# 48 gate tiles as 24 pairs of seven block products, computed ahead of attention and kept in DRAM

## The chip, the cores and the metric

The kernel runs on one core of a Trainium2 chip. What counts is the device time of one execution in microseconds (us); the time before is the median of three runs. Durations of single instructions come from one profiled execution.

## What is computed

One step of a hybrid decoder layer for 512 tokens of a prompt and 64 sample tokens (8 sequences of 8), which share all weights. Everything is float32. Cut to what matters here:

```python
h = _rmsnorm(x, norm_w)
u = jnp.einsum('bld,de->ble', h, w_in)         # D_MODEL = 2048 rows, all projections at once
z = u[..., OFF_Z:OFF_XBC]                      # 4096 columns
...                                            # xbc (6144), dt (64), q (2048), k and v (512 each)
g_attn = u[..., OFF_GA:OFF_MIX_S]              # 2048 columns
mix_s, mix_a = ...                             # 2048 columns each
y = _gated_group_rmsnorm(ssd(conv(xbc), dt), z, ssm_norm_w)   # y * silu(z), then a norm by group
p_ssm = y @ w_ssm_branch
o = sink_attention(q, k, v, bias) * jax.nn.silu(g_attn)
p_attn = o @ w_attn_branch
merged = jax.nn.sigmoid(mix_s) * p_ssm + jax.nn.sigmoid(mix_a) * p_attn
x = x + merged @ w_out                         # then a last rmsnorm
```

So z and g_attn are used only through a SiLU, at the end of the state-space part and of attention. Of the input projection's columns, z and g_attn are 48 tiles of 128.

## The kernel before

Tokens lie along the free dimension: 576 columns, in two halves of TH = 288. A projection tile has 128 output columns; its weights, 2048 rows, come in two chunks of 8 k-tiles (128x8x128, 512 KB, loaded by SyncE in L63 into `raw`, two buffers). `Weights.split` makes two parts of a chunk that TensorE takes at full rate, whose sum is the float32 value: `wh` by ScalarE (L70) and `wl` by VectorE (L71), three buffers each. The activations are kept in such parts too (`ah`, `al`). For each k-tile, `step` in `run_main` issues three products (wh with ah, wh with al, wl with ah) on two token halves: 6 matmuls of 288 columns, 96 a tile, all in L338, each half onto a PSUM bank of its own (`ps` in pool `pm`, two buffers of two banks).

`run_main` walks a list of tiles. After each k-tile it calls `pump`, which lets one step of the oldest generator in `quick` and one of the oldest in `jobs` issue its instructions. In this way attention (`attn_job`, about 117 steps for one of four rounds of eight heads), the convolution and the state-space groups (`ssd_job`) run between the matmuls of the projections: the engines' order is the order in which these steps are issued. If the list ends first, `drain` runs the rest without matmuls beside it.

The order of tiles: four of K, four of V, dt; then for each attention round m four tiles of q, some mix gates (`MIXES` = 6, 6, 6, 8) and the four attention gates ga of that round (`take_ga`, SiLU on ScalarE). The round's `attn_job` starts with its last q tile; at its end it waits for the ga tiles, multiplies on GpSimd (L551) and stores the result to `o_d` (L553). Then for each of eight state-space groups six tiles of xbc and four of z (`take_z`, L750, kept in SBUF as `zs`), the six mix gates that are left, and after these the output projections of the two branches and `w_out` (two parts of 320 and 256 tokens).

In a block of `attn_job`, the scores (L493) are reduced with the bias by VectorE (L497), the maximum is negated (`nm`, L504), ScalarE takes eight exponentials (L509), VectorE scales by the sum (L516), and TensorE transposes the result (L526) for the product with V (L536). Tables and constants, among them the bias expanded to DRAM (`bias_d`, eight issues of GpSimd in L370) and copies of the two caches (L409), are set up at the start, and their transfers run during K and V.

Of the kernel before, what the change touches and what calls it, by code (L numbers as in the profile page):

```python
# [16 lines left out]
P = 128  # L17
# [28 lines left out]
MIXES = (6, 6, 6, 8)  # L46
# [8 lines left out]
class Weights:  # L55
    """Weight tiles of 8 k-tiles x 128 columns, each split into two float32r parts."""
# [19 lines left out]
def hybrid(ctx, tc, x_prompt, x_sample, cache_k, cache_v, state_conv, state_ssm, norm_w, w_in, conv_w,  # L76
# [32 lines left out]
    sink_d = scratch([HEADS, 8], "sink_d")  # L109
    ea_d = scratch([H, T], "ea_d")  # L110
# [53 lines left out]
    # parameters that scale rows of transposed tiles  # L164
# [42 lines left out]
    hx, first = [act_pair(k) for k in range(KT)], []  # L207

    def to_hx(k, lo, hi, blocks):
# [43 lines left out]
    open_pools(True)  # L253

    def stat(n, name):
        return now["s"].tile([P, n], F32, tag=name, name=name)

# [1 line left out]
    pool.dma_start(out=tri, in_=c_tri)  # L259
    pool.dma_start(out=stri, in_=c_stri)  # L260
    pool.dma_start(out=own, in_=c_own)
    pool.dma_start(out=sinkb, in_=AP(sinks, 0, [[0, P], [1, HEADS]]))
    dska = kten([P, H], "dska")
    pool.dma_start(out=dska, in_=AP(d_skip, 0, [[0, P], [1, H]]))
    for hf in range(2):
        pool.tensor_copy(dsk[64 * hf:64 * hf + 64, :],
                         dska[64 * hf:64 * hf + 64].rearrange("p (t h) -> p t h", h=2)[:, :, hf])
    rb = now["s"].tile([HEADS, HEADS], F32, tag="rb", name="rb", bufs=1)
    oh = kten([P, BL], "oh")
    bd = kten([P, BL], "bd")  # L270
    pool.dma_start(out=rb, in_=rel_bias)
    pool.dma_start(out=oh[:32], in_=c_buckets)
    pool.dma_start(out=bd[:32], in_=c_band)
    pbk = bank()
    ten.matmul(pbk[:32, :BL], rb, oh[:32], start=True, stop=True)
    vec.tensor_tensor(out=oh[:32], in0=pbk[:32, :BL], in1=bd[:32], op=ALU.add)
    pool.dma_start(out=AP(biass_d, 120, [[3056, 32], [383, 8], [1, 143]]),
                   in_=AP(oh, 120, [[oh.ap[0][0], 32], [0, 8], [1, 143]]))
    sk = now["s"].tile([HEADS, 1], F32, tag="sk", name="sk", bufs=1)
    pool.dma_start(out=sk, in_=sinks.rearrange("a h -> h a"))  # L280
    sk8 = now["s"].tile([HEADS, 8], F32, tag="sk8", name="sk8", bufs=1)
    pool.tensor_copy(sk8, sk.to_broadcast([HEADS, 8]))
    pool.dma_start(out=sink_d, in_=sk8)
    for b2 in range(2):
        pool.dma_start(out=sinks_s[64 * b2:64 * b2 + 64], in_=AP(sink_d, 0, [[1, 64], [64, 4]]))

# [11 lines left out]

    def pump():
        pump_one(quick)  # L300
        pump_one(jobs)
# [9 lines left out]
    def run_main(tiles, had=()):  # L311
        """tiles: (weight loads per chunk of 8 k-tiles, act pairs, what takes the sums[, the only tokens]).
        With had, the first chunks of the first two tiles, those two tiles run side by side."""
# [11 lines left out]
        def step(n, kk, only=(0, 1)):  # L325
            i, c = flat[n]
            loads, pairs, take, *spans = tiles[i]
# [28 lines left out]

    win = w_in[0]
# [81 lines left out]
    gaT = {}  # L439
# [16 lines left out]
    def take_ga(m, r):  # L456
        def f(ps):
            gaT[m, r] = cten("ga")
            act.activation(sq(gaT[m, r]), ps[:, :, :TH], AF.Silu)
        return f  # L460

    def attn_job(m):
# [6 lines left out]
        # keys of the two kv heads, high and low parts, each twice  # L469
# [75 lines left out]
        for blk in range(4):  # L545
            yield from scores(blk)
        yield from sample_attn(m, oT)
        while (m, 3) not in gaT:
            yield
        for t in range(4):  # L550
            pool.tensor_tensor(out=oT[t], in0=oT[t], in1=gaT.pop((m, t)), op=ALU.mult)  # L551
# [113 lines left out]
        # dt in x_; dt * A, cumulated within chunks and sequences  # L665
# [11 lines left out]
        # decay to the end, times dt  # L677
# [106 lines left out]
    def ssd_job(g):  # L784
# [4 lines left out]
        # masked C.B, B by token  # L789
# [67 lines left out]
        yield from wait(2)  # L857
        yield from ssd_sample(g, xs, bT, cT)
        # gate and group norm
        tot = cten("tot")  # L860
        sqr = cten("sqr")
        for t in range(4):
            vec.tensor_tensor(out=xs[t], in0=xs[t], in1=zs.pop(4 * g + t), op=ALU.mult)  # L863
# [24 lines left out]
    def parts(dst, src, q, high, low):  # L888
        """The 32 rows of src (from partition 32 q on): high and low parts to those quarters of dst."""
# [370 lines left out]
```

## Time and profile before

| | us |
|---|---|
| median of three runs (lowest, highest) | 3341.83 (3338.98, 3344.56) |
| span of the profiled execution | 3334.8 |
| TensorE busy | 3246.0 (97%) |
| VectorE busy | 1526.2 (46%) |
| ScalarE busy | 1266.9 (38%) |
| GpSimd busy | 348.7 (10%) |

The profiled execution's own time isn't listed apart; its span runs from its first to its last instruction, and the timed runs also hold what lies around it. Shares are means over stages: the projections' matmuls run through the whole span, while attention ends at about 1106 us and the state-space groups, some 163 us each, come after it.

### The profile page before, as it was taken

Reading aid. Unit: us, or ns where it says so; the run is one execution under the profiler, and the core shown is the slowest. Engines: PE = TensorE matmul, PEld = TensorE weight load, DVE = VectorE, ACT = ScalarE, POOL = GpSimd, SP = SyncE. Lnnn points to the kernel's source line nnn. Section 1 sums busy time; section 2 is a strip of 40 time slices with the busy share of each in tenths; the row PEclk is TensorE's granted clock in tenths of the full one; section 3 lists DMA queues with packets and bytes.
Section 4 is the critical chain, followed back from the end, with each engine's and each line's share of the span. In section 5 each row is a group of like instructions: output and inputs, shape, how many; then the busy total and the mean of one; then the engine's idle time right before and its main releaser. Section 6 shows DMA issues by size and latency. Waiting matters only on the chain.

```text
span 3334.8 us, 57384 instructions
## 1 busy us (share of the span) xinstructions
PE 3246.0 (97%) x23897; PEld 3086.3 (93%) x23897; DVE 1526.2 (46%) x2881; ACT 1266.9 (38%) x2153; POOL 348.7 (10%) x423
## 2 busy tenths in 40 slices
PE   7499999999999999999999999999999999999997
PEld 6499998999999999999999898989899999999997
DVE  4044233243242375757575757575642242423544
ACT  4035335254262344444444444444431121211443
POOL 4000100100000012121212120202010000000111
PEclk9799999999999999999999999999999999999999
DMA  5933333233323344435353535353574353433555
GB/s 138 148 103 93 93 99 95 84 91 88 103 81 99 97 124 114 130 109 131 106 135 105 136 101 141 100 139 96 143 233 122 108 163 105 146 108 97 158 156 160
DMA packets 667924, 398.39 MB, mean 119 GB/s; under 512 B 31248, under 2 KB 638704, under 8 KB 667472
## 3 DMA queue, kind: packets, MB, share of 16 engines
q1 hardware_dynamic: 660800, 383.93, 40.8%
q0 software_dynamic: 6864, 10.79, 2.4%
q8 instruction: 188, 3.08, 0.4%
q14 instruction: 72, 0.59, 0.1%
HBM read 339.24 MB, written 59.29 MB: 120 GB/s over the span
## 4 chain that ended last, share of the span: by engine, by line
PE 86%; DMA 6%; POOL 3%; DVE 2%; ACT 2%; issue 1%; SPq 0%; DVEq 0%; ACTq 0%; POOLq 0%
PE ps L338 74%; PE bank L974 2%; DMA raw<-in_w_out_dram 2%; DMA raw<-in_w_in_dram 2%; PE bank L759 1%; PE bank L536 1%; POOL tot L867 1%; DMA out_dram<-knp 1%; PE bank L493 1%; PE bank L953 1%; DMA stg<-y_d 1%; POOL sqr L865 1%; PE bank L827 1%; PE bank L526 1%; DVE wl L71 1%
## 5 line engine op out<-in xcount | busy, mean ns | idle before, releaser
L338 PE MATMUL ps<-ah,wh 128*128 128x288 f32 (+2 forms) x6944 | 1568.5, 300 | 28.8 <-ACT wh L70 27.1
L338 PE MATMUL ps<-ah,wl 128*128 128x288 f32 (+2 forms) x6944 | 1554.4, 298 | 2.0 <-DVE wl L71 2.0
L338 PE MATMUL ps<-al,wh 128*128 128x288 f32 (+2 forms) x6944 | 1545.4, 297 | 0.0
L338 PEld LDWEIGHTS ps<-ah,wh 128*128 128x128 f32 x6944 | 1136.2, 190 | 65.4 <-issue 31.9
L338 PEld LDWEIGHTS ps<-ah,wl 128*128 128x128 f32 x6944 | 1138.7, 189 | 25.9 <-issue 19.9
L338 PEld LDWEIGHTS ps<-al,wh 128*128 128x128 f32 x6944 | 1138.3, 189 | 15.1 <-issue 13.2
L71 DVE TENSOR_TENSOR wl<-raw,wh 128x1024 fp32r<-128x1024 f32 x466 | 582.4, 1251 | 1107.2 <-ACT wh L70 1105.9
L70 ACT ACTIVATE wh<-raw 128x1024 fp32r<-128x1024 f32 x466 | 492.7, 1058 | 1364.6 <-PE ps L338 1125.8
L730 DVE SCALAR_TENSOR_TENSOR cacc<-craw,prm,cacc 128x600 f32<-128x600 f32 x144 | 128.5, 892 | 61.2 <-ACT cacc L728 57.8
L1179 POOL TENSOR_TENSOR res<-res,fw 128x128 f32<-128x128 f32 (+3 forms) x35 | 32.4, 949 | 856.7 <-ACT junk L1175 824.9
L968 DVE SCALAR_TENSOR_TENSOR s<-s,dec_s,bank 128x128 f32<-128x128 f32 x256 | 70.4, 343 | 59.5 <-PE bank L962 59.2
L497 DVE CUSTOM_DVE_ANT_0 sc<-bank,bm 128x256 f32<-128x256 f32 (+1 forms) x128 | 43.8, 388 | 85.0 <-PE bank L493 83.9
L773 DVE TENSOR_SCALAR L<-L,acs_n 128x128 f32<-128x128 f32 (+1 forms) x320 | 79.2, 322 | 5.9 <-DMA L<-acs_d 5.4
L1125 DVE TENSOR_TENSOR sg<-ps,sg 128x576 f32<-128x576 f32 x32 | 24.3, 758 | 124.7 <-PE ps L338 124.7
L815 POOL TENSOR_TENSOR xl<-xe,xh 128x512 fp32r<-128x512 f32 x32 | 42.2, 1320 | 260.3 <-ACT xh L814 233.2
L509 ACT ACTIVATE sc<-sc,nm 128x256 f32<-128x256 f32 (+1 forms) x128 | 60.0, 470 | 21.7 <-DVE nm L504 16.9
L865 POOL TENSOR_TENSOR tot<-xc 128x576 f32<-128x576 f32 x8 | 32.6, 4069 | 310.0 <-DVE xc L863 310.0
L974 PE MATMUL bank<-sT,cpad 128*32 128x512 f32 x128 | 61.7, 603 | 1.9 <-ACT sT L955 1.9
L955 ACT ACTIVATE sT<-bank 128x512 f32<-128x512 f32 x64 | 36.4, 598 | 68.1 <-PE bank L953 67.9
L725 POOL COPY g<-craw 128x3 f32<-128x3 f32 x48 | 38.0, 791 | 216.2 <-ACT craw L713 215.8
L541 ACT ACTIVATE oT<-bank 64x128 f32<-64x128 f32 x128 | 34.9, 272 | 46.6 <-PE bank L536 45.3
L775 ACT ACTIVATE L<-L 128x512 f32<-128x512 f32 (+1 forms) x80 | 45.2, 584 | 16.8 <-DVE L L773 15.6
(293 smaller groups left out, 2372.8 us busy)
## 6 DMA issues: line engine op xcount, KB each, us to landing
raw<-in_w_in_dram SPq DMA_DIRECT2D x306, 512.0 KB
raw<-in_w_ssm_branch_dram SPq DMA_DIRECT2D x64, 512.0 KB
raw<-in_w_out_dram SPq DMA_DIRECT2D x64, 512.0 KB
L<-acs_d SPq DMA_DIRECT2D x64, 256.0 KB
s<-in_state_ssm_dram SPq DMA_DIRECT2D x64, 256.0 KB
out_dram<-s SPq DMA_DIRECT2D x64, 256.0 KB
raw<-in_w_attn_branch_dram SPq DMA_DIRECT2D x32, 512.0 KB
y_d<-xc SPq DMA_DIRECT2D x32, 288.0 KB
```

Of the source, the lines that this page charges most:

```text
L70: pin(nc.scalar.activation(wh, raw, AF.Copy))
L71: pin(nc.vector.tensor_tensor(out=wl, in0=raw, in1=wh, op=ALU.subtract))
L338: ten.matmul(sums[i][:, s, :hi - lo], a[:, kk, :], b[:, lo:hi], start=(k == 0 and q == 0), stop=(k == last and q == 2))
L497: vec.tensor_tensor_reduce(out=s_[:, i, lo:256], in0=ps[:, i, lo:256], in1=bm[j][:, i, lo:256], scale=1.0, scalar=-3e38, op0=ALU.add, op1= ...
L509: act.activation(sc[j][:, i, lo:256], sc[j][:, i, lo:256], AF.Exp, bias=nm[:, h:h + 1], accum_out=sm[:, h:h + 1])
L730: vec.scalar_tensor_tensor(out=acc[:, :600], in0=raw[:, i:i + 600], scalar=prm[:, i * 48 + j:i * 48 + j + 1], in1=acc[:, :600], op0=ALU.mu ...
L773: vec.tensor_scalar(out=l_[:rows, i, :n], in0=l_[:rows, i, :n], scalar1=acs_n[:rows, blk, h:h + 1], scalar2=0.0, op0=ALU.subtract, op1=ALU ...
L775: act.activation(l_[:rows, :, :n], l_[:rows, :, :n], AF.Exp)
L815: pool.tensor_tensor(out=xl, in0=xe, in1=xh, op=ALU.subtract)
L865: pool.tensor_tensor(out=dst, in0=xs[t], in1=xs[t], op=ALU.mult)
L968: vec.scalar_tensor_tensor(out=sts[i][:, t, :], in0=sts[i][:, t, :], scalar=dec_s[:, 4 * g + t, b:b + 1], in1=ps[:, v, i, :], op0=ALU.mult ...
L974: ten.matmul(pyo[32 * bl:32 * bl + 32, :], cpad[:, 4 * hb + bl, :], sTs[i], start=True, stop=True, tile_position=(0, 32 * bl))
```

## The change

Two neighbouring tiles of a gate (256 columns of weights) times the activations are seen as a product of 2x2 blocks: weights A11, A12, A21, A22 (128 columns of 1024 rows: the second digit is the half of the rows, the first the tile) with activations split by half of the rows and half of the tokens. Strassen's way, in Winograd's form, takes seven block products in place of eight, with sums of blocks ahead and behind.

- The kernel starts with six mix tiles (`FIRST`) in place of K. During them `sums_job` forms the sums of activation blocks: for each of 8 k-tiles four additions, four subtractions and three splits into parts, on 128x288. One block (`b12`) is overwritten by its sum `t1` after the mix tiles and put back from DRAM (`xb_d`) in the last pair.
- `run_pairs` then makes the 48 tiles of ga and z as 24 pairs. A pair loads four chunks (L363), VectorE forms S1 to S4 of them (L376, 128x1024), seven chunks are split (L75, L76), and each product is 24 matmuls of 128x288 (L436) onto one bank. Products 4, 5 and 6 add onto the banks of products 0, 2 and 3. `evict` adds with the other products (L390) or takes the bank as it is, and `gate_out` applies the SiLU and stores to `ga_d` or `z_d`, with DMAs issued by ScalarE (L1090).
- Tables and constants are set up after the pairs; then K, V, dt and the four attention rounds follow with `MIXES` = 1, 1, 1, 5 mix tiles and no ga tile. `pump` calls `jobs` 12/8 times a step there. The gates are read back from `ga_d` ahead of the sample part of a round.
- A state-space group has its six tiles and one or two mix tiles (`MIXES_S`) instead of four z tiles; `zs` is read back from `z_d`. Six mix tiles are left at the end as before.

On TensorE, in the first attention round, the stream's matmuls between the last scores of its fourth block and the first transposes were these. The transposes are those that write `bank` from `ident` and `sc`. Before, at the end of the scores:

```order
L493 MATMUL bank<-kh,qs 128x256
L493 MATMUL bank<-kl,qs 128x256
L493 MATMUL bank<-kh,qs 128x256
L493 MATMUL bank<-kl,qs 128x256
L338 MATMUL ps<-ah_231,wh 128x288 x2
L338 MATMUL ps<-al_232,wh 128x288 x2
```

The scores end here and the stream (L338) goes on alone. TensorE again, 32 rows further, where the first transposes stand:

```order
L338 MATMUL ps<-al_222,wh 128x288 x2
L338 MATMUL ps<-ah_221,wl 128x288 x2
L338 MATMUL ps<-ah_223,wh 128x288
L526 MATMUL bank<-ident,sc 128x128 x9
L338 MATMUL ps<-ah_223,wh 128x288
L526 MATMUL bank<-ident,sc 128x128
```

The transposes come after 73 matmuls of the stream.

After, on TensorE at the same place, the end of the scores (L572; the stream is L332):

```order
L332 MATMUL ps<-ah_248,wl 128x288
L572 MATMUL bank<-kh,qs 128x256
L572 MATMUL bank<-kl,qs 128x256
L572 MATMUL bank<-kh,qs 128x256
L572 MATMUL bank<-kl,qs 128x256
L332 MATMUL ps<-ah_248,wl 128x288
L332 MATMUL ps<-ah_250,wh 128x288 x2
L332 MATMUL ps<-al_251,wh 128x288 x2
```

The scores end one row later in the stream's k-tile. TensorE again, nine rows of two matmuls further, where the transposes (L605) stand:

```order
L332 MATMUL ps<-ah_224,wl 128x288 x2
L332 MATMUL ps<-ah_226,wh 128x288 x2
L332 MATMUL ps<-al_227,wh 128x288
L605 MATMUL bank<-ident,sc 128x128 x16
L332 MATMUL ps<-al_227,wh 128x288
```

There were 73 matmuls of the projections between the two, and now there are 28.

On VectorE, at the end of the first attention round, during its four ga tiles, there stood before (`wl` is the low part of a chunk of weights, `qs` a q tile's parts):

```order
L624 COPY pw<-bank 64x512
L71 TENSOR_TENSOR wl<-raw,wh 128x1024
L635 COPY oT<-bank 64x64 x8
L71 TENSOR_TENSOR wl<-raw,wh 128x1024 x8
L448 SCALAR_TENSOR_TENSOR qs<-ps,qs 64x576 x2
L71 TENSOR_TENSOR wl<-raw,wh 128x1024 x2
L448 SCALAR_TENSOR_TENSOR qs<-ps,qs 64x576 x2
```

Eight `wl` in a row belong to the four ga tiles and nothing stands between them.

VectorE where ga and z are made now, in the middle of a pair (`u`, `w`, `c` are sums of products, L376 forms S1, S3, S2 of the next pair, in this order):

```order
L390 TENSOR_TENSOR u<-ps,p_1660 128x288
L76 TENSOR_TENSOR wl<-raw,wh 128x1024
L376 TENSOR_TENSOR raw<-raw 128x1024
L390 TENSOR_TENSOR w<-ps,u 128x288
L376 TENSOR_TENSOR raw<-raw 128x1024
L76 TENSOR_TENSOR wl<-raw,wh 128x1024
L390 TENSOR_TENSOR w<-ps,w 128x288
L376 TENSOR_TENSOR raw<-raw 128x1024
L76 TENSOR_TENSOR wl<-raw,wh 128x1024 x2
L390 TENSOR_TENSOR c<-ps,u 128x288
L76 TENSOR_TENSOR wl<-raw,wh 128x1024
```

Sums of whole chunks and of products now stand among the `wl` of a pair.

The diff, cut to its core:

```diff
-MIXES = (6, 6, 6, 8)
+FIRST = 6
+MIXES = (1, 1, 1, 5)
+MIXES_S = (2, 1, 2, 1, 2, 1, 2, 1)
...
 def pump():
     pump_one(quick)
-    pump_one(jobs)
+    pace["at"] += pace["rate"]
+    while pace["at"] >= 8:
+        pace["at"] -= 8
+        pump_one(jobs)
...
+def run_pairs(cols, ops, takes, after=None):
...
+    for p in range(n):
+        for i in range(7):
+            if i < 5:
+                split(p, i + 2)
+            else:
+                split(p + 1, i - 5)
+            if i == 1:
+                load(p + 1, "A11", "A21", "A22")
+            elif i == 2:
+                sum_(p, "S4")
+            elif i == 3:
+                sum_(p + 1, "S1")
+                load(p + 1, "A12")
+            elif i == 4:
+                sum_(p + 1, "S2")
+            elif i == 5:
+                sum_(p + 1, "S3")
...
+            for k in range(8):
+                ah, al = ops[i][k]
+                for q, (a, b) in enumerate(((wh, ah), (wh, al), (wl, ah))):
+                    ten.matmul(st[p]["ps", i][:, :TH], a[:, k, :], b, start=i < 4 and k == 0 and q == 0,
+                               stop=k == 7 and q == 2, skip_group_check=i >= 4)
+                pump()
+            evict(p, i)
...
 # attn_job
-        while (m, 3) not in gaT:
-            yield
+        ga = [cten("ga") for _ in range(4)]
+        for t in range(4):
+            sync.dma_start(out=ga[t], in_=ga_d[(4 * m + t) * P:(4 * m + t + 1) * P, :])
         yield from sample_attn(m, oT)
...
 # ssd_job
+        zs = [cten("zs") for _ in range(4)]
+        for t in range(4):
+            sync.dma_start(out=zs[t], in_=z_d[(4 * g + t) * P:(4 * g + t + 1) * P, :])
         yield from ssd_sample(g, xs, bT, cT)
...
+    def gate_out(func, dst, n):
+        def f(j, src, t_):
+            act.activation(t_, src, func)
+            act.dma_start(out=dst[n * P:(n + 1) * P, j * TH:(j + 1) * TH], in_=t_)
+        return f
...
+    quick.append(sums_job())
+    run_main([m_in(c, by_halves(gate_out(AF.Sigmoid, d_, n))) for c, d_, n in mixes[:FIRST]], first)
+    drain()
+    ops[2] = [split_half(b12[k], t1[k]) for k in range(8)]
...
+    run_pairs(cols, ops, takes, b12_again)
...
     for m in range(4):
-        seq += m_q(m) + left[:MIXES[m]] + m_ga(m)
+        seq += m_q(m) + left[:MIXES[m]]
         del left[:MIXES[m]]
-    run_main(seq, first)
+    pace["rate"] = 12
+    run_main(seq)
+    pace["rate"] = 8
...
-        for t in range(4):
-            seq.append(m_in((4 * g + t) * P, take_z(4 * g + t)))
+        seq += left[:MIXES_S[g]]
+        del left[:MIXES_S[g]]
```

## Rows read from the trace of the kernel before

**Rows 1.** The page: span; busy time of each engine, its share and instructions; the chain of work that ended last, by engine and by line.

```profile
span 3334.8 us, 57384 instructions
...
PE 3246.0 (97%) x23897; PEld 3086.3 (93%) x23897; DVE 1526.2 (46%) x2881; ACT 1266.9 (38%) x2153; POOL 348.7 (10%) x423
...
PE 86%; DMA 6%; POOL 3%; DVE 2%; ACT 2%; issue 1%; SPq 0%; DVEq 0%; ACTq 0%; POOLq 0%
PE ps L338 74%; PE bank L974 2%; DMA raw<-in_w_out_dram 2%; DMA raw<-in_w_in_dram 2%; PE bank L759 1%; PE bank L536 1%; POOL tot L867 1%; DMA out_dram<-knp 1%; PE bank L493 1%; PE bank L953 1%; DMA stg<-y_d 1%; POOL sqr L865 1%; PE bank L827 1%; PE bank L526 1%; DVE wl L71 1%
```

**Rows 2.** The waits of TensorE: what waited for what, us in total, times, longest.

```profile
PE ps L338 <- ACT wh L70: 27.1, 3, 16.6
PE bank L392 <- ACT kT L380: 19.1, 1, 19.1
PE bank L214 <- DVE x L190: 10.2, 5, 5.8
PE bank L195 <- DMA nwr<-in_norm_w_dram: 5.7, 1, 5.7
PE bank L1163 <- ACT ot L1154: 5.0, 4, 2.8
```

**Rows 3.** The chain of waits between 60 and 200 us: start, us, what it went through.

```profile
72.18 38.11 DMA raw<-in_w_in_dram
...
113.35 33.46 DMA out_dram<-knp
...
170.18 12.79 PE ps L338 x96
...
183.52 12.80 PE ps L338 x96
```

**Rows 4.** The same chain in the out projection, near the end: start, us, what.

```profile
3151.06 7.04 PE ps L338 x48
...
3215.01 4.20 DMA raw<-in_w_out_dram
...
3229.02 6.12 DMA raw<-in_w_out_dram
...
3237.57 4.75 DMA raw<-in_w_out_dram
```

**Rows 5.** Instructions grouped by line, engine, operation and shape over the whole span: after the first bar busy us and mean ns of one, after the second the idle time ahead of them and what ended it.

```profile
L71 DVE TENSOR_TENSOR wl<-raw,wh 128x1024 fp32r<-128x1024 f32 x466 | 582.4, 1251 | 1107.2 <-ACT wh L70 1105.9
L70 ACT ACTIVATE wh<-raw 128x1024 fp32r<-128x1024 f32 x466 | 492.7, 1058 | 1364.6 <-PE ps L338 1125.8 <-DMA raw<-in_w_out_dram 85.9 <-DMA raw<-in_w_in_dram 72.0
...
L1062 DVE TENSOR_TENSOR al<-stg,ah 128x576 fp32r<-128x576 f32 x48 | 34.5, 755 | 17.4 <-ACT ah L1061 17.1
...
L509 ACT ACT_TABLE_LOAD x15 | 19.2, 1283 | 8.6 <-DVE nm L504 8.4
...
L712 ACT ACTIVATE craw<-ps 128x288 f32<-128x288 f32 x48 | 18.9, 393 | 0.0
...
L1166 DVE TENSOR_TENSOR res<-bank,res 128x128 f32<-128x128 f32 x64 | 15.4, 282 | 6.2 <-PE bank L1163 6.2
```

**Rows 6.** Stretches of the span: from and to, length, then busy us of TensorE, its weight loads, VectorE, ScalarE and GpSimd with their instructions, the granted clock of TensorE, the DMA engines' busy share, GB/s.

```profile
21.00:61.00 40.00, 39.95 (x264) 35.59 (x264) 25.16 (x53) 21.47 (x45) 11.00 (x10) 1.00 0.28 71
70.00:115.00 45.00, 25.89 (x186) 25.63 (x185) 4.49 (x4) 5.90 (x10) 5.51 (x8) 0.79 0.96 108
115.00:165.00 50.00, 26.17 (x170) 25.14 (x170) 3.82 (x6) 4.31 (x7) 2.17 (x4) 0.77 0.85 167
606.00:824.00 218.00, 218.00 (x1584) 206.40 (x1584) 72.19 (x190) 91.42 (x190) 11.06 (x17) 0.99 0.32 93
1560.00:1723.00 163.00, 162.48 (x1201) 149.95 (x1200) 102.08 (x190) 72.79 (x120) 29.05 (x34) 1.00 0.44 120
2440.00:2680.00 240.00, 240.00 (x1848) 240.00 (x1848) 79.11 (x80) 58.84 (x68) 0.00 (x0) 1.00 0.49 149
384.00:390.00 6.00, 6.00 (x26) 5.88 (x27) 1.78 (x8) 0.00 (x0) 1.42 (x1) 0.54 0.12 49
```

**Rows 7.** DMA between 60 and 180 us: the software queue (packets, MB, share of the 16 engines), and an issue of GpSimd's (number, KB of each, median us to landing).

```profile
q0 software_dynamic: 6410, 10.52, 65.2%
...
bias_d<-oh POOLq DMA_DIRECT2D x8, 766.0 KB, 42.9
```

**Rows 8.** The timeline of all engines in the fourth block of the first attention round, from its last score on: start, us, engine, line, operation.

```profile
335.87 0.28 PE L493 MATMUL bank<-kl,qs 128*128 128x256 f32 x1
...
337.20 0.17 DVE L504 TENSOR_SCALAR nm<-mx 128x8 f32<-128x8 f32 x1
...
337.84 1.28 ACT L509 ACT_TABLE_LOAD   x1
...
342.70 0.50 ACT L509 ACTIVATE sc<-sc,nm 128x256 f32<-128x256 f32 x1
...
343.76 0.36 DVE L516 TENSOR_SCALAR sc<-sc,sm 128x256 f32<-128x256 f32 x1
```

**Rows 9.** The timeline of GpSimd at the end of the last attention round, in brackets the idle time ahead and what ended it.

```profile
1101.11 1.93 POOL L551 TENSOR_TENSOR oT<-oT,ga 128x576 f32<-128x576 f32 x1 [10.87 <-ACT ga L459]
```

**Rows 10.** The chain of waits at the same place.

```profile
1103.07 3.32 DMA o_d<-oT
```

More of the change, by code (lines that the diff above doesn't have):

```diff
@@ L206, in hybrid, with parts_of, to_hx @@
     normed(order[4], pin)
-    hx, first = [act_pair(k) for k in range(KT)], []
-    def to_hx(k, lo, hi, blocks):
+    hk = [act_pair(k) for k in range(KT)]
+    hb = [[[[t[:, j * TH:(j + 1) * TH] for t in hk[8 * i + k]] for k in range(8)] for j in range(2)] for i in range(2)]
+    first = []
+    def parts_of(dst, src, nw):
+        ah, al = dst
+        act.activation(ah, src, AF.Identity, scale=nw)
+        vec.scalar_tensor_tensor(out=al, in0=src, scalar=nw, in1=ah, op0=ALU.mult, op1=ALU.subtract)
+    def to_hx(k, blocks):
+        lo = blocks[0] * P if 0 in blocks else 256
         ps = bank()
@@ L251, in kten @@
         return now["k"].tile(shape, dt, tag=now["kt"], name=name)
[L253 to L285, printed above, removed]
     jobs, quick = [], []
@@ L326, in step @@
             i, c = flat[n]
-            loads, pairs, take, *spans = tiles[i]
+            loads, pairs, take = tiles[i]
             last = len(loads) * 8 - 1
@@ L1017, in hybrid @@
-    mixes = [m_in(OFF_MA + n * P, take_mix(ma_d, n)) for n in range(16)]
-    mixes += [m_in(OFF_MS + n * P, take_mix(ms_d, n)) for n in range(16)]
+    hx = [[[hb[k // 8][j][k % 8][part] for j in range(2)] for part in range(2)] for k in range(KT)]
+    stk = ExitStack()
+    tx, rs, ev = (stk.enter_context(tc.tile_pool(name=n_, bufs=b_, reuse_waits="tile"))
+                  for n_, b_ in (("tx", 1), ("rs", 5), ("ev", N_E)))
+    b12, t1 = hb[0][1], []
+    ops = [hb[0][0], [], [], [], hb[1][0], hb[1][1], []]
@@ new lines, in hybrid, with b12_again @@
+    back = []
+    def b12_again(i):
+        if i == 1:
+            for k in range(8):
+                back.append(ev.tile([P, TH], F32, tag="e", name="x"))
+                sync.dma_start(out=back[k], in_=xb_d[k * P:(k + 1) * P, :])
+        elif i == 2:
+            for k in range(8):
+                split_half(b12[k], back[k])
+    run_pairs(cols, ops, takes, b12_again)
+    stk.close()
+    ms.close()
+    pm = ctx.enter_context(tc.tile_pool(name="pm", bufs=2, space=PSUM, reuse_waits="tile"))
@@ new lines, in hybrid, with stat @@
+    open_pools(True)
+    def stat(n, name):
+        return now["s"].tile([P, n], F32, tag=name, name=name)
+    pool.dma_start(out=tri, in_=c_tri)
+    pool.dma_start(out=stri, in_=c_stri)
+    pool.dma_start(out=own, in_=c_own)
+    pool.dma_start(out=sinkb, in_=AP(sinks, 0, [[0, P], [1, HEADS]]))
+    dska = kten([P, H], "dska")
+    pool.dma_start(out=dska, in_=AP(d_skip, 0, [[0, P], [1, H]]))
+    for hf in range(2):
+        pool.tensor_copy(dsk[64 * hf:64 * hf + 64, :],
+                         dska[64 * hf:64 * hf + 64].rearrange("p (t h) -> p t h", h=2)[:, :, hf])
@@ new lines, in hybrid @@
+    rb = now["s"].tile([HEADS, HEADS], F32, tag="rb", name="rb", bufs=1)
+    oh = kten([P, BL], "oh")
+    bd = kten([P, BL], "bd")
+    pool.dma_start(out=rb, in_=rel_bias)
+    pool.dma_start(out=oh[:32], in_=c_buckets)
+    pool.dma_start(out=bd[:32], in_=c_band)
+    pbk = bank()
+    ten.matmul(pbk[:32, :BL], rb, oh[:32], start=True, stop=True)
+    vec.tensor_tensor(out=oh[:32], in0=pbk[:32, :BL], in1=bd[:32], op=ALU.add)
+    pool.dma_start(out=AP(biass_d, 120, [[3056, 32], [383, 8], [1, 143]]),
+                   in_=AP(oh, 120, [[oh.ap[0][0], 32], [0, 8], [1, 143]]))
@@ L1020, in hybrid @@
+    sk = now["s"].tile([HEADS, 1], F32, tag="sk", name="sk", bufs=1)
+    pool.dma_start(out=sk, in_=sinks.rearrange("a h -> h a"))
+    sk8 = now["s"].tile([HEADS, 8], F32, tag="sk8", name="sk8", bufs=1)
+    pool.tensor_copy(sk8, sk.to_broadcast([HEADS, 8]))
+    pool.dma_start(out=sink_d, in_=sk8)
+    for b2 in range(2):
+        pool.dma_start(out=sinks_s[64 * b2:64 * b2 + 64], in_=AP(sink_d, 0, [[1, 64], [64, 4]]))
     seq = [m_in(OFF_K + i * P, take_k(i)) for i in range(4)]
```

153 lines of the change are left out of this document (119 added, 34 removed).

## The prediction

> **What bounds the kernel now.** I read the page first [rows 1]: TensorE is busy for 97% of the span and holds 86% of the chain that ended last, 74% of it in one line, L338, the projections. VectorE (46%) and ScalarE (38%) are shares over stages, so I went on to the waits of TensorE [rows 2]: they come to some 75 us, and the four large ones lie at the start (normalizing x) and in one flood of transfers between 70 and 165 us, not in the projections' steady state. The chain between 60 and 200 us [rows 3] shows both: a weight load that took 38.11 us, and, after it, tiles at full speed, 96 matmuls of 288 columns in 12.79 us, 133.2 ns each. The windows [rows 6] then say stage by stage what else is near its limit: at 606:824 (one of four attention rounds) TensorE is busy throughout and ScalarE 42%, at 1560:1723 (one of eight groups of the state-space part) VectorE is at 63%. So a removed matmul is worth its 133.2 ns as long as what remains still covers the other engines' chains. The span is 3334.8 us, the median of the timed runs 3341.8: 7.0 us lie around the span, which I keep.
>
> **What goes: matmuls.** 48 gate tiles cost 48 x 96 = 4608 matmuls; 24 pairs by seven products of 24 cost 4032. The 576 that go are 576 x 133.2 ns = **76.7 us**. That holds if a product, whose 24 matmuls all add onto one bank, runs at the old rate; the old stream changes banks at each matmul. The out projection is the nearest row [rows 4]: its 48 matmuls of 320 columns on one bank took 7.04 us, 0.458 ns a column, against 133.2 / 288 = 0.463. Each of the page's matmuls has its own weight load already (equal counts, [rows 1]), so using a weight half as often adds none. I take the old rate; the other end, 0.458, would give only 5 us more over 4032 matmuls.
>
> **What is added: sums on VectorE.** An addition of two 128x288 tiles has no row. Between 128 columns at 282 ns and 576 at 755 ns [rows 5] a line gives 282 + 160 x 1.056 = 0.45 us. The Trainium skill, "VectorE: DVE Perf Modes", section on why tensor_tensor can't do 2x_2P or 4x, says that such a float32 addition of two tensors gets no faster mode; its formula there, (N + 151) / 0.96 ns, would give an estimate of 0.46 us. The trace agrees at 576 columns (755 ns against 757).
>
> *Start.* From 21 us to the end of the six mix tiles at about 112 us, VectorE has: the old work of 21:61, 25.2 us [rows 6]; eight further wl of 1.251 us, 10.0; the 88 additions, 39.7; 16 more small evictions, some 3; eight splits for product 2, 3.6; the first pair's three sums and two wl, 6.3. Together 88 of 91 us. That just fits on average, but the additions start only at the 36th step, where a chunk's 6.4 us hold one wl and about 5.5 us of additions. So the last ones can run over. I take 4 us; the bounds are 0 (the three wl buffers absorb it) and 15 (all that comes after the last tile in series: the splits, the sums and wl, a few late additions).
>
> *Pairs.* TensorE needs 7 x 24 x 133.2 ns = 22.4 us for a pair. VectorE: 7 wl and 4 sums of a whole chunk, 11 x 1.251 = 13.8, and 5 additions, 2.3: 16.0 us. ScalarE: 7 wh of 1.058, five of about 0.39 and four DMA issues: about 11. Both have room, so the question is a chain. Counted from the end t of product 0: wh and wl of product 3 free the buffer of the next pair's A21 (t + 2.85, with ScalarE's copy of product 0 ahead); its load lands; S1 (1.25), an addition (0.45), S3 (1.25) and then wl of product 5 (1.25) stand on VectorE in that order (the section on the change has its rows). If S1 waits for the load, everything behind it waits too, and TensorE is the one that needs that wl, at t + 12.8 (four products of 3.2). With a landing of 4.2 us it is done at t + 11.3, with 6.1 us at t + 13.2 (both landings in [rows 4]): room of 1.5 us, or 0.4 short. Over 24 pairs that is 0 to 10 us; I take 3, nearer to the shorter landings, because at 2440:2680, where the projections load without a pause, TensorE never waited [rows 6] and the pairs ask for less than those 149 GB/s (2.7 MB in 22.4 us, 120 GB/s).
>
> **What is moved.** *Attention.* Ten mix tiles' and all gate tiles' matmuls leave each round: 14 tiles in 218 us [rows 6] become 5 (64 us) in about 103, and a round's own TensorE work stays at 218 - 179 = 39 us. What the tiles covered is the softmax between a block's last score and its first transpose. In the trace that chain runs from 336.0 us (last score) over the maximum (337.2), a table load of 1.28, eight exponentials and the scaling to 344.1 [rows 8]: 8.1 us, and 6.4 without the table load and the wh that stood ahead of it. Counted from the order of TensorE's instructions, the stream's matmuls in that gap were 62, 71, 77, 73 for the four blocks. They become 62, 71, 69, 28 in the first round, 64, 76, 46, 31 in the second and third, 64, 76, 77, 67 in the last. 6.4 us are 48 matmuls, 8.1 us are 61. So 28 leaves TensorE idle for 2.7 to 4.4 us, 31 for 2.3 to 4.0 (twice), 46 for 0.3 to 2.0 (twice): **8 to 16 us**. Blocks 2 and 3 have no table load ahead of their exponentials in the new order; I take 9.
>
> *Into the state-space part.* Before, the last round ended with gate tiles, and the gating on GpSimd was spread under them [rows 9]. Now the sample part is the last thing: four multiplies of 1.93 us each, after them a store of 3.32 us [rows 10], before the pools are free: with the copies some 12.3 us, and about 15 until the first convolution's rows land. TensorE holds one tile, 12.8 us. I take 2 us (0 to 5).
>
> *State space.* A group falls from 10 tiles to 7.5, from 163.6 to 131.6 us; VectorE's 102 us become about 96 (5 wl fewer), 73% on average and, where one group's scan overlaps the next one's convolution, above 100% for a while. I take 3 us (0 to 16).
>
> *The flood.* Eight bias expansions and eight cache copies [rows 7] move behind the pairs, unchanged. In 70:165 TensorE was busy for only 52 of 95 us [rows 6], and of the 43 idle, 19.1 and a 16.6 are named waits [rows 2]. The same transfers now meet K's second chunk and the tiles after it, with some 30 us of work in hand where 26 stood. I take no change, with 10 us either way. The 14 MB each way of stored gates lie in stages with room (shares of 0.32 and 0.44 of the DMA engines, [rows 6]): nothing.
>
> **Sum.** In the profiled span: 3334.8 - 76.7 + (4 + 3 + 9 + 2 + 3) = 3279; with the 7.0 around it **3286 us**. All lower bounds and the flood's gain give 3263, all upper ones 3337.
>
> **Rivals.**
> (1) TensorE is bound everywhere, the softmax gaps are filled by work that I count as late, and only the 76.7 us show: 3265. For it: the waits in steady state are nearly nil today [rows 2]. Against it: 28 matmuls are 3.7 us, and the exponentials alone take longer.
> (2) The clock falls in the stalls. At 384:390, in a thin stretch of attention, the granted clock was 0.54 [rows 6], that is about the lower of the two levels (1.2 GHz); 6 us there did 46% less. If five attention stalls, and four more among the transition and the state-space part, each cost such a dip, 9 x 2.8 = 25 us come on top: 3311. The Trainium skill, "TensorE: Matmul & The Clock Gate", section "HAM oscillation", tells of just that: idle between tiles puts the engine back to the slow clock, so that each next tile starts cold. In the trace it happened where the idle was long (0.79 and 0.77 in the flood [rows 6]), while most short waits left 1.00.
> (3) Slower: the pairs are bound by the A21 chain. Each us of landing beyond 5.7 costs 24 us in all. Without the pairs' 3 us I have 3283, so at 5.7 + 58.8 / 24 = 8.2 us the gain is gone, and at 9 us it would be 3283 + 24 x 3.3 = 3362. For it: in the flood a load took 38.11 us [rows 3], and here ScalarE's stores and the next A12 are in flight beside A21. The Trainium skill, "DMA: Bandwidth & Descriptors", section "Issuing engines are not separate DMA queues", says that a store issued from another engine still interleaves with the loads on the same 16. Against it: the landings of 4.2 to 6.1 us come from a stage that already loads and stores side by side, and the pairs move less.
> (4) The change does not do what it says, if one bank's accumulation were slower: 5% on 4032 matmuls is 27 us, 3313; the out projection's row speaks against it, and I count it with (2).
>
> **How the numbers follow.** Forecast (3270 to 3300): 0.57. Rival 1: 0.12. Rival 2 and 4 (3300 to 3320): 0.19. Rival 3: 0.12, of which 0.05 still end faster, 0.03 the same, 0.04 slower. The range from 3266 to 3314 leaves out a third of rival 1, a fifth of 2, and 3. A measurement of this kernel can tell about 0.2% (6.7 us) from no change: faster 0.12 + 0.57 + 0.19 + 0.05 = 0.93, same 0.03, slower 0.04.
>
> **What would show it.** Right: pair matmuls at 22.4 to 23 us a pair, with waits on the line of wl under 1 us a pair; in attention, waits of TensorE for the scaled scores at the blocks with 28 and 31 matmuls, none at the others; a wait of about 2 us at the first convolution; flood idles near 43 us. Wrong: waits for A21 under S1 above 2 us a pair (rival 3), granted clock under 0.95 over the attention rounds (rival 2), or a flood that costs twice or nothing.

## The result

| | us |
|---|---|
| before, median of seven runs (lowest, highest) | 3340.73 (3338.29, 3346.31) |
| changed, median of seven runs (lowest, highest) | 3351.51 (3349.81, 3352.75) |
| ratio changed to before, 95% interval | 1.0025 (1.0015 to 1.0036) |

The change made the kernel slower by some 0.25%. The forecast was 3286 us, with a range from 3266 to 3314; the time lies above its end, and above 3337, the sum of all upper bounds. Of all timed runs in this document one, the tenth of the experiment with the small q copy, ran at a granted clock of 0.62 and took 4681.9 us; the median given there is that of the other nine. The page of the changed kernel, with the lines that answer to [rows 1]: span, busy time, the chain that ended last by engine.

```profile
span 3350.6 us, 57391 instructions
...
PE 3207.2 (96%) x23321; PEld 3041.5 (91%) x23321; DVE 1812.0 (54%) x3289; ACT 1328.3 (40%) x2325; POOL 338.3 (10%) x431
...
PE 84%; DMA 7%; DVE 3%; ACT 3%; POOL 1%; issue 1%; SPq 1%; DVEq 0%; ACTq 0%; POOLq 0%
```

576 matmuls are gone (23897 to 23321), yet TensorE's busy time fell by only 39 us and the span rose by 16. So there is new idle time, and some matmuls took longer. The waits of TensorE (what waited for what, us in total, times, longest), against [rows 2]:

```profile
PE bank L478 <- ACT kT L466: 35.2, 2, 26.9
PE ps L332 <- ACT q L536: 28.2, 6, 6.0
PE ps L332 <- ACT wh L75: 15.6, 3, 12.5
PE bank L233 <- DVE x L199: 12.2, 6, 6.1
PE ps L332 <- ACT mix L1079: 11.8, 7, 2.8
```

The first, third and fourth row are the flood and the start, which stood there before. New are the second and the fifth: the projection stream itself (`ps`, L332) waits for ScalarE to copy a q or a mix tile out of PSUM. No row names the transposes, where I had put the stalls. Stage by stage (columns as in [rows 6]):

```profile
0.00:119.00 119.00, 96.82 (x658) 90.01 (x659) 87.44 (x206) 62.87 (x134) 28.00 (x32) 0.99 0.51 145
119.00:654.00 535.00, 534.47 (x4036) 534.24 (x4034) 361.53 (x388) 223.50 (x299) 0.00 (x0) 1.00 0.43 121
654.00:770.00 116.00, 67.73 (x463) 65.90 (x464) 12.79 (x11) 14.81 (x23) 16.20 (x22) 0.79 0.85 141
888.00:1394.00 506.00, 462.12 (x2997) 409.69 (x2997) 199.86 (x691) 241.61 (x632) 36.46 (x73) 0.90 0.30 85
1400.00:2484.00 1084.00, 1079.13 (x7949) 979.41 (x7948) 760.20 (x1474) 506.62 (x877) 224.42 (x264) 1.00 0.53 143
```

The pairs (second row) are TensorE's alone: 0.5 us idle in 535. In the chain of waits they are one piece:

```profile
119.44 534.04 PE ps L436 x4032
```

That is 132.45 ns a matmul, and 22.25 us a pair. The state-space part (fifth row) is idle for 4.9 us. What is left is attention (fourth row): TensorE idle for 43.9 of 506 us, and a mean clock of 0.90. The same stretch before, four rounds from the first scores to the last sample product, had no idle time at all:

```profile
266.00:1036.00 770.00, 770.00 (x5570) 722.98 (x5569) 261.33 (x729) 339.21 (x725) 36.64 (x64) 0.99 0.32 92
```

I call **loss** what a stage has of TensorE's idle time, plus busy time x (1 - granted clock). Summed over stretches of 2 us, so that slow clock in idle time is not counted twice:

| loss, us | before | changed |
|---|---|---|
| start | 17.9 | 23.7 |
| pairs | | 0.5 |
| flood of transfers | 49.4 | 53.8 |
| attention, first scores to last sample product | 10.9 | 85.4 (43.9 idle, 41.5 clock) |
| state-space part | 4.1 | 4.9 |
| output projections | 24.3 | 26.1 |

The differences add up to 88, of which attention is 74. With the 76.7 us of removed matmuls that makes +11; the spans differ by 15.8, and some 5 us are not found in this account.

One of the stops, on ScalarE in the second round (timeline: start, us, engine, line, operation, in brackets the idle time ahead and what ended it):

```profile
950.46 2.26 ACT L620 ACTIVATE oT<-bank 64x128 f32<-64x128 f32 x8 [5.34 <-PE bank L615]
952.75 0.65 ACT L532 ACTIVATE qs<-ps 64x576 fp32r<-64x576 f32 x1
953.96 1.06 ACT L75 ACTIVATE wh<-raw 128x1024 fp32r<-128x1024 f32 x1 [0.56 <-PE ps L332]
955.03 0.65 ACT L532 ACTIVATE qs<-ps 64x576 fp32r<-64x576 f32 x1
955.71 0.51 ACT L588 ACTIVATE sc<-sc,nm 128x256 f32<-128x256 f32 x1
...
959.65 0.19 ACT L585 ACTIVATE es<-es 128x8 f32<-128x8 f32 x1
959.87 0.22 ACT L536 ACTIVATE q<-ps 128x64 f32<-128x64 f32 x1
```

And TensorE at that time:

```profile
931.68 0.42 PE L332 MATMUL ps<-ah,wl 128*128 128x288 f32 x2
933.91 0.53 PE L332 MATMUL ps<-ah,wh 128*128 128x288 f32 x2 [1.80 <-ACT q L536]
...
953.75 0.42 PE L332 MATMUL ps<-ah,wl 128*128 128x288 f32 x2
960.14 0.85 PE L332 MATMUL ps<-ah,wh 128*128 128x288 f32 x2 [5.97 <-ACT q L536]
960.79 0.68 PE L332 MATMUL ps<-al,wh 128*128 128x288 f32 x2
```

A q tile ended at 932.1. Its first copy out of PSUM ran at 952.8, because the output copies of a block (L620) stand ahead of it on ScalarE, and these waited 5.3 us for the product with V. Its last one, 0.22 us long, stood behind eight exponentials and ran at 959.9. The next tile of the stream fills the other PSUM tile and ends at 954.2; then neither is free, and TensorE stops for 6 us. After the stop two matmuls take 0.68 us and more instead of 0.42: the clock has fallen to its lower level (1.2 GHz) and comes back at about 964.5. In a window over this place it is 0.62:

```profile
957.00:966.00 9.00, 5.86 (x31) 5.86 (x32) 4.26 (x19) 3.46 (x15) 0.10 (x1) 0.62 1.00 292
```

### The profile page after: what moved, and what is told of

Its sections match the earlier page's. It is cut to its first block, busy times and chain, and to the rows that moved or that the text cites. A ratio compares the mean times of both kernels' runs of the same rounds, so it can differ in the third digit from the quotient of the medians.

```text
span 3350.6 us, 57391 instructions
## 1 busy us (share of the span) xinstructions
PE 3207.2 (96%) x23321; PEld 3041.5 (91%) x23321; DVE 1812.0 (54%) x3289; ACT 1328.3 (40%) x2325; POOL 338.3 (10%) x431
## 4 chain that ended last, share of the span: by engine, by line
PE 84%; DMA 7%; DVE 3%; ACT 3%; POOL 1%; issue 1%; SPq 1%; DVEq 0%; ACTq 0%; POOLq 0%
PE ps L332 56%; PE ps L436 16%; DMA raw<-in_w_in_dram 3%; DMA raw<-in_w_out_dram 2%; PE bank L1049 2%; PE bank L615 1%; DMA L<-acs_d 1%; DVE wl L76 1%; PE bank L831 1%; ACT wh L75 1%; PE bank L1028 1%; PE bank L572 1%; PE bank L605 1%; PE bank L899 1%; PE bank L895 0%
## 5 line engine op out<-in xcount | busy, mean ns | idle before, releaser
L332 PE MATMUL ps<-ah,wh 128*128 128x288 f32 (+2 forms) x5408 | 1242.2, 302 | 59.2 <-ACT q L536 28.2
L332 PE MATMUL ps<-ah,wl 128*128 128x288 f32 (+2 forms) x5408 | 1240.0, 301 | 3.2 <-DVE wl L76 3.2
L332 PE MATMUL ps<-al,wh 128*128 128x288 f32 (+2 forms) x5408 | 1237.7, 301 | 0.0
L76 DVE TENSOR_TENSOR wl<-raw,wh 128x1024 fp32r<-128x1024 f32 x538 | 672.6, 1251 | 831.6 <-ACT wh L75 787.8
L75 ACT ACTIVATE wh<-raw 128x1024 fp32r<-128x1024 f32 x538 | 570.0, 1060 | 1296.9 <-PE ps L332 781.3
L332 PEld LDWEIGHTS ps<-ah,wh 128*128 128x128 f32 x5408 | 901.9, 192 | 79.8 <-ACT q L536 29.5
L332 PEld LDWEIGHTS ps<-al,wh 128*128 128x128 f32 x5408 | 904.7, 192 | 27.6 <-issue 26.0
L332 PEld LDWEIGHTS ps<-ah,wl 128*128 128x128 f32 x5408 | 902.4, 192 | 26.9 <-issue 20.2
L436 PE MATMUL ps<-ah,wl 128*128 128x288 f32 x768 | 226.2, 295 | 0.0
L436 PE MATMUL ps<-ah,wh 128*128 128x288 f32 x768 | 226.2, 294 | 0.0
L436 PE MATMUL ps<-al,wh 128*128 128x288 f32 x768 | 226.1, 294 | 0.0
L436 PEld LDWEIGHTS ps<-al,wh 128*128 128x128 f32 x768 | 144.1, 188 | 0.0
L436 PEld LDWEIGHTS ps<-ah,wl 128*128 128x128 f32 x768 | 144.0, 188 | 0.0
L436 PEld LDWEIGHTS ps<-ah,wh 128*128 128x128 f32 x768 | 144.0, 188 | 0.0
L376 DVE TENSOR_TENSOR raw<-raw 128x1024 f32<-128x1024 f32 x96 | 117.0, 1220 | 27.3 <-DMA raw<-in_w_in_dram 26.4
```

Source lines behind the costliest of these rows:

```text
L75: pin(nc.scalar.activation(wh, raw, AF.Copy))
L76: pin(nc.vector.tensor_tensor(out=wl, in0=raw, in1=wh, op=ALU.subtract))
L332: ten.matmul(sums[i][:, s, :part.shape[1]], a[:, kk, :], part, start=(k == 0 and q == 0), stop=(k == last and q == 2))
L376: vec.tensor_tensor(out=s_[x], in0=s_[a], in1=s_[b], op=op)
L436: ten.matmul(st[p]["ps", i][:, :TH], a[:, k, :], b, start=i < 4 and k == 0 and q == 0, stop=k == 7 and q == 2, skip_group_check=i >= 4)
```

## The experiments

My theory (A): attention's steps now come too densely, 1.5 to a k-tile of the stream with 5 tiles a round where 14 stood, so the chain through the engines' fixed orders can't keep up, the stream's two PSUM tiles stay full, and each stop costs the clock as well. Rivals: (B) it is the place, since q tiles now run beside a softmax and before they ran after it; (C) the total of matmuls in a round counts, whatever the steps' density. The ratios below are to the kernel before, run on the same chip.

**More tiles in attention, steps as dense as before.**

```diff
-MIXES = (1, 1, 1, 5)
-MIXES_S = (2, 1, 2, 1, 2, 1, 2, 1)
+MIXES = (3, 3, 3, 8)
+MIXES_S = (1, 0, 0, 1, 0, 0, 1, 0)
...
-    pace["rate"] = 12
+    pace["rate"] = 8
```

> The changed kernel with attention at 8/8 steps a k-tile (as before the change) instead of 12/8, and with mix tiles moved from the state-space part to attention so that the steps still find matmuls beside them: MIXES = 3, 3, 3, 8 and MIXES_S with three tiles in all. The number of matmuls is the same. Theory A (attention's steps are packed too densely, so that ScalarE's queue and the two PSUM tiles of the stream run out; each stop also drops the clock): the 85 us of idle and slow clock in the attention rounds fall to 25 or less, TensorE's wait for the q tiles' copies from 28 us to under 5, the total to about 3290 us. Theory B (it hurts that q tiles of the next round now lie beside a round's softmax, at any rate): the wait for the q copies stays at 20 us or more, total 3325 or more. Either way the state-space groups, with 6 to 7 tiles instead of 7 to 8, may lose up to 15 us.

Measured: 3343.0 us, ratio 1.0006 (0.9997 to 1.0015). Attention, and the state-space part:

```profile
888.00:1412.00 524.00, 524.00 (x3668) 474.08 (x3667) 217.60 (x694) 266.73 (x652) 37.08 (x68) 0.97 0.35 101
1424.00:2486.00 1062.00, 1005.15 (x7311) 906.98 (x7311) 739.30 (x1478) 509.18 (x882) 221.26 (x267) 0.97 0.50 138
```

In attention no us is idle, and the wait for q copies is gone, as theory A has it (loss 15 us); B would have kept it. But the total hardly moved: the state-space part, now with 6.4 tiles a group, is idle for 56.8 us and loses 75. I had allowed it 15. Its largest wait:

```profile
PE bank L880 <- ACT xc L812: 26.2, 6, 8.8
```

The SiLU behind the convolution (L812) waits for VectorE's part of it: VectorE is busy throughout five of these six stops, and for 5.4 of 6.1 us in the sixth.

**The same tiles, steps at 12/8.** The edit is the one above without its last two lines.

> The same move of mix tiles into attention, but at 12/8 steps a k-tile as in the changed kernel. Theory A (density of the steps): stops and slow clock stay where the softmax runs, since as many matmuls as now stand between its steps; total within 15 us of the changed kernel, 3335 to 3365. Theory C (too few matmuls in a round as a whole, whatever their spread): as good as at 8/8, about 3290.

Measured: 3359.5 us, ratio 1.0061 (1.0044 to 1.0078). Attention, and the state-space part:

```profile
885.00:1412.00 527.00, 502.59 (x3466) 451.21 (x3464) 207.05 (x690) 264.27 (x647) 32.29 (x68) 0.96 0.32 93
1450.00:2504.00 1054.00, 1005.47 (x7315) 905.59 (x7313) 742.52 (x1470) 506.77 (x880) 226.86 (x269) 0.98 0.50 139
```

In attention 24.4 us idle and a loss of 43, against 15 with the same tiles at 8/8: that is the density of the steps alone. It isn't all, as the loss is half of the changed kernel's 85. Theory C, taken alone, falls; A was too strong in expecting the stops to stay where they were. The state-space part loses 64 here, with the same tiles as in the run at 8/8, so the total is the largest so far.

**The small q copy on VectorE.**

```diff
-            act.activation(q0, ps[:, 1, 512 - TH:TH], AF.Copy, scale=0.125)
+            vec.tensor_scalar(out=q0, in0=ps[:, 1, 512 - TH:TH], scalar1=0.125, scalar2=None, op0=ALU.mult)
```

> The changed kernel with one instruction moved: the last small copy of a q tile (128x64 out of PSUM, 0.22 us on ScalarE) is done by VectorE. In the longest stop this copy stood behind eight exponentials (4 us) on ScalarE, and TensorE waited for it. If ScalarE's order is what holds the PSUM tile (theory A or B), the wait named for the q copies falls from 28 to 15 us or less and the total by 10 to 30 us, to 3320 to 3340, with the first two copies of a q tile as the next limit. If the tile is late for another reason, nothing changes (within 5 us).

Measured: 3343.9 us, ratio 1.0010 (1.0001 to 1.0020). That is 8 us less than the changed kernel, or 5 by the two ratios, whose intervals overlap; in either case a smaller gain than expected. The wait is now named after the copy on its new engine:

```profile
PE ps L332 <- DVE q L536: 22.0, 8, 4.8
```

It fell from 28.2 to 22.0, not to 15. The place behind the exponentials is a part of the delay. That the larger one is ahead of it, in the copies that wait for the product with V, fits the stop shown above, but no run took those copies away.

**Before, with q tiles beside the softmax.**

```diff
+    seq += m_q(0)
     for m in range(4):
-        seq += m_q(m) + left[:MIXES[m]] + m_ga(m)
+        seq += (m_q(m + 1) if m < 3 else []) + left[:MIXES[m]] + m_ga(m)
```

> The kernel before, with only the order of tiles changed: the next round's four q tiles come right behind a round's own, so that they run beside its softmax, at 8/8 steps a k-tile; the gates stay where they were and as many matmuls are done as before. Theory B (q tiles beside the softmax are the fault): waits for the q copies of some 20 us and a slower clock, 3370 or more. Theory A (density): no such wait worth 5 us, 3335 to 3350.

Measured: 3345.6 us, ratio 1.0016 (1.0007 to 1.0025). Attention:

```profile
266.00:1046.00 780.00, 780.00 (x5611) 730.44 (x5610) 267.38 (x732) 319.69 (x712) 33.54 (x64) 0.98 0.33 92
```

No idle time, and no wait for a q copy. So B falls: the place does no harm where one step goes with a k-tile, here with 14 tiles a round and in the run with more tiles in attention with 7.

**Steps at 10/8.**

```diff
-MIXES = (1, 1, 1, 5)
-MIXES_S = (2, 1, 2, 1, 2, 1, 2, 1)
+MIXES = (2, 2, 2, 5)
+MIXES_S = (1, 1, 1, 1, 1, 1, 1, 2)
...
-    pace["rate"] = 12
+    pace["rate"] = 10
```

> Between the changed kernel and its variant with 8/8 steps: 10/8 steps of attention a k-tile, MIXES = 2, 2, 2, 5 and one mix tile in most state-space groups. The earlier runs showed that the loss only moved: 85 us in attention and 5 in the state-space part at 7.5 tiles a group, 15 and 75 at 6.4 tiles a group with 8/8 steps. If the losses grow the faster the fewer matmuls cover a stage (theory A, widened: both stages together have too few matmuls), the middle is cheaper than both ends: some 35 us in attention and 20 in the state-space part, total 3310 to 3330. If the sum of cover is all that counts, the loss stays near 90 us wherever the tiles are: 3340 to 3350.

Measured: 3315.2 us, ratio 0.9931 (0.9919 to 0.9944). Attention and the state-space part:

```profile
888.00:1362.00 474.00, 471.08 (x3271) 422.34 (x3271) 206.01 (x687) 250.52 (x639) 38.49 (x74) 0.97 0.34 100
1362.00:2450.00 1088.00, 1050.04 (x7671) 951.40 (x7670) 746.11 (x1482) 509.56 (x883) 216.99 (x266) 0.98 0.51 138
```

Losses of 18 and 52 us, where I had 35 and 20: the total lies in its range, its split doesn't. One more tile a round and 10/8 steps take nearly all of attention's loss away. The state-space part loses more than I thought at 7.1 tiles a group, while 7.5 lose 5. In the changed kernel a group takes about 131 us almost without idle time, and 7 tiles give 7 x 12.8 + 35.6 = 125; I took the 131 for a floor, the time that a group's other engines need. Two halves of the stretch, cut where the fourth group's product with the mask begins (L866), say otherwise:

```profile
1362.00:1810.00 448.00, 445.83 (x3294) 408.23 (x3293) 305.42 (x585) 213.24 (x382) 86.26 (x115) 1.00 0.49 131
1810.00:2450.00 640.00, 604.21 (x4379) 543.17 (x4378) 440.69 (x898) 296.32 (x502) 130.73 (x151) 0.97 0.52 143
```

The first half loses 3 us and the second 49. In the run with 8/8 steps it is 3 up to the fourth group and 72 from there on, and its last groups, with 6 tiles between them, follow one another after 121 to 125 us. So 131 us is no floor, and the loss isn't a fixed price for each group: the first groups pass with few tiles, the later ones pay. Why it begins there is open.

**Repeated tiles in the state-space part.** It adds five mix tiles that are computed twice to the first of these kernels.

```diff
+    again = [m_in(c, take_mix(d_, n)) for c, d_, n in mixes[FIRST:FIRST + 8]]
...
+        if g in (1, 2, 4, 5, 7):
+            seq.append(again[g])
```

> The variant with 8/8 steps (15 us lost in attention, 75 in the state-space part), with five mix tiles computed a second time in the groups that had none: 480 matmuls, 64 us of work that the result does not need. Theory A (the state-space groups wait for want of matmuls beside VectorE's chain): the loss there falls from 75 to 30 or less, so that the kernel is only 5 to 25 us slower than without the repeats (3343), 3348 to 3368. If the groups' loss has another cause (traffic, say), the 64 us come on top: 3400 or more.

Measured: 3381.0 us, ratio 1.0136 (1.0117 to 1.0156): 38 us more than without the repeats, for 64 us of matmuls. The time lies between the two forecasts. The state-space part:

```profile
1424.00:2515.00 1091.00, 1053.70 (x7720) 955.30 (x7719) 743.85 (x1475) 509.61 (x883) 221.14 (x268) 0.98 0.51 138
```

Its loss fell from 75 to 47, not to 30. So about 26 us of needless work were hidden in stops, as A says in part; the groups still stop at 7 tiles, as the run with 10/8 steps also showed.

**Only z in pairs.** ga's tiles are whole tiles again in their rounds (`take_ga` as before), 16 pairs are left:

```diff
-    for off, dst, m in ((OFF_GA, ga_d, D // P), (0, z_d, DI // P)):
+    for off, dst, m in ((0, z_d, DI // P),):
...
-        seq += m_q(m) + left[:MIXES[m]]
+        seq += m_q(m) + left[:MIXES[m]] + m_ga(m)
```

> Only z's 32 tiles are made as 16 pairs; the 16 attention gates are again whole tiles at the end of each attention round, as before the change, at 8/8 steps a k-tile, with MIXES = 0, 0, 0, 4 and two mix tiles in each state-space group. It saves 16 x 24 = 384 matmuls, 51 us. Eight tiles (128 steps) cover a round's 117 steps and eight a group. Theory A: no stops in attention beyond the 11 us before the change, state-space loss under 10: 3340 - 51 + 6 (start) + 4 (transfers) = 3299, 3290 to 3310. If the pairs or the way through DRAM cost something that I took for attention's loss, it stays above 3320.

Measured: 3306.2 us, ratio 0.9903 (0.9890 to 0.9917), as A had it. Attention, and the state-space part:

```profile
700.00:1260.00 560.00, 560.00 (x3957) 509.68 (x3956) 223.31 (x705) 280.58 (x668) 35.52 (x67) 0.98 0.31 87
1282.00:2434.00 1152.00, 1144.91 (x8403) 1042.24 (x8402) 787.53 (x1490) 532.63 (x911) 234.69 (x270) 1.00 0.52 139
```

In attention nothing is idle and the loss is 14; the state-space part loses 7. So the pairs and the way through DRAM bring what they should where the stages behind them keep their matmuls.

**22 pairs.** Two pairs of z less; their four tiles go into attention, at 10/8 steps, and the state-space groups have 7.6 tiles each.

```diff
-    for off, dst, m in ((OFF_GA, ga_d, D // P), (0, z_d, DI // P)):
+    for off, dst, m in ((OFF_GA, ga_d, D // P), (0, z_d, DI // P - 4)):
...
-    left = [m_in(c, take_mix(d_, n)) for c, d_, n in mixes[FIRST:]]
+    left = [m_in(n * P, take_zd(n)) for n in range(28, 32)] + [m_in(c, take_mix(d_, n)) for c, d_, n in mixes[FIRST:]]
```

with `MIXES` = 2, 2, 2, 5 and `MIXES_S` = 2, 1, 2, 1, 2, 1, 2, 2; `take_zd` applies the SiLU and stores to `z_d`.

> 22 pairs instead of 24: z's last four tiles are whole tiles again (384 matmuls for two pairs' 336, 6.4 us more) and lie in attention, at 10/8 steps a k-tile with 11 tiles beside the four rounds' q tiles, as in the run with 10/8 steps, while the state-space groups get 13 mix tiles, 7.6 tiles a group, as in the changed kernel. The run with 10/8 steps lost 18 us in attention and 52 in the state-space part (7.1 tiles a group); the changed kernel 5 in the state-space part (7.5 tiles). Theory A with a floor of some 131 us a group: 3315 + 6 - 47 = 3275, 3265 to 3290. If the state-space part's loss comes from the denser work of attention ahead of it, or from the shift in time, it stays: 3310 or more.

Measured: 3290.0 us, ratio 0.9858 (0.9842 to 0.9875), the fastest of all, at the upper end of what I expected. Attention and the state-space part:

```profile
845.00:1318.00 473.00, 470.18 (x3267) 421.06 (x3266) 205.57 (x686) 252.46 (x645) 38.61 (x74) 0.97 0.35 100
1318.00:2416.00 1098.00, 1093.22 (x8063) 994.23 (x8063) 772.62 (x1488) 516.02 (x891) 227.12 (x266) 1.00 0.53 142
```

Losses of 16 and 5 us. (The profiled execution is the fastest of four, 3282.2 us; the others took 3288.9 to 3291.1.) The same denser steps in attention ahead of it (10/8) leave the state-space part alone once it has its tiles, so its 52 us in the earlier run were for want of tiles.

## Why the prediction was wrong

- *Matmuls, -76.7 us*: right. 4032 took 534.04 us, 132.45 ns each; one bank for a product cost nothing, so rival 4 is out. Of the 70.3 us that 22 pairs save, the kernel with them shows 48 at the end.
- *Start, +4 (0 to 15)*: the loss rose by 5.8 us. Right.
- *Pairs, +3 (0 to 10)*: 0.5 us idle in the whole stage. Right, at its lower end, and rival 3, my only road to a slower kernel, did not happen: VectorE's sums waited 26.4 us for loads, 1.1 us a pair, but TensorE never did.
- *Flood, 0 (10 either way)*: +4.4. *Transition, +2*: 0.1 us idle there (1394:1424). *State space, +3 (0 to 16)*: +0.8. Right.
- *Attention, +9 (8 to 16)*: **this step failed**; it measured 74. I reckoned one chain only, from a block's last score to its first transpose, and set the stream's matmuls in that gap against it. TensorE named no wait at the transposes. The chain is longer: scores, softmax, transposes, copies, product with V, output copies, and again the next block, and ScalarE works all of it in one fixed order together with the stream's own copies out of PSUM. With 5 tiles a round these copies came up to 20 us late, two PSUM tiles were not enough, and TensorE stopped for 28 us on q tiles and 10 on mix tiles in attention (43.9 us with all others).
- *The clock* belongs to that step in part: 41.5 us of the 85 are matmuls at the lower clock, 31 more than before. About 23 of them lie in and behind the stops. The other 19 lie in the four rounds' sample parts, where nothing was idle, and such places held all of the 10.9 before; the prediction's own row 384:390 [rows 6] is one, with 6.00 of 6 us busy. Rival 2 had the mechanism of the 23, with nine dips of 2.8 us (25 us); its place and the idle time ahead of the dips were wrong, so its 3311 was still far too low. The Trainium skill, "TensorE: Matmul & The Clock Gate", section "HAM oscillation", tells that a wait puts the engine back to the slow clock and that what comes next starts cold; here the trace agrees, with 0.62 over the 9 us from 957.
- What I took as the bound of that term, "8 to 16", was the bound of one mechanism. Busy shares would not have warned me: ScalarE was at 42% in a round before (91 of 218 us, [rows 6]) and is at 46% in the changed kernel's second round (57 of 123), so no engine is full, and yet the round took 123 us and not 103.

```profile
957.00:1080.00 123.00, 110.89 (x708) 97.86 (x708) 50.40 (x173) 57.04 (x154) 8.43 (x18) 0.89 0.29 83
```

That the loss comes from too few matmuls beside the other engines' work is shown: it went from attention to the state-space part when tiles went the other way and attention's steps were spread (85 and 5, 15 and 75), it was small in both at once when two pairs were given up (16 and 5, against 18 and 52 with the same steps and all pairs), and needless matmuls were partly free. What is not settled: how much of attention's loss is the order on ScalarE and how much the length of the chain. Moving the one small copy took away 5 to 8 us; more PSUM tiles for the stream were not tried, since all eight banks are in use. In the state-space part it is not settled why the first groups lose almost nothing. Nor was it tried why the account is 5 us short.

## What to carry to other kernels

Matmuls that are taken out of a stage are gained only as long as those that remain still cover the longest chain through the other engines, and that chain is a whole round of work on engines that keep their order, not the one gap that waits today. Before moving work out of such a stage, find out how little cover it still runs on without stops, and over the whole stage, since here the first groups hid the lack (the state-space part lost 5 us at 7.5 tiles a group and 52 at 7.1; attention stood idle for 44 us at 5 tiles a round with 12/8 steps and for 3 at 6 with 10/8), and stop there: spreading the steps and moving tiles turned 0.25% slower into 0.7% faster, and giving up 2 of 24 pairs as well made it 1.4%. Take the gain where nothing hides behind the matmuls, and leave the cover where something does.

## What the hardware showed that I had not expected

- A stop of 6 us costs some 2 us more: behind it, from 960.1 to 964.5, the clock was at its lower level, and two matmuls took 0.68 us instead of 0.42. In attention some 23 us were lost in this way beside 43.9 us of idle time.
- The clock falls without any idle time too: in each round's sample part, with its 64-column products, TensorE counts as busy all the time and the clock was at 0.63 over 14 us in three rounds, at 0.72 over 12 us in the last. At 8/8 steps, before the change, it fell in the same parts ([rows 6], 384:390).

```profile
996.00:1010.00 14.00, 14.00 (x66) 12.75 (x66) 6.88 (x24) 2.10 (x3) 5.53 (x4) 0.63 0.24 85
1120.00:1134.00 14.00, 14.00 (x67) 12.87 (x67) 6.86 (x29) 1.34 (x2) 5.52 (x4) 0.63 0.19 68
1242.00:1256.00 14.00, 14.00 (x65) 12.70 (x65) 6.88 (x24) 2.30 (x3) 5.53 (x4) 0.63 0.27 92
1368.00:1380.00 12.00, 12.00 (x62) 11.29 (x62) 3.15 (x9) 1.06 (x1) 6.54 (x4) 0.72 0.17 59
```

- Too little cover shows late: with 7.1 tiles a group the state-space part lost 3 us up to the fourth group and 49 from there on.
